# An encoder trunk on one core: the recurrence's squares summed before PE, row loads and top-k begun earlier, and the last tile's output on two engines

## The chip, the core and the metric

The kernel runs on one core of a Trainium2 chip. PE multiplies matrices, DVE and ACT work elementwise, POOL (GpSimd) here mostly issues gathers, SP issues loads and stores; the core shares 16 DMA engines among all of them. The metric is the time of one execution in microseconds (us). Before the change the median of three runs is 1483.56 us (1481.76 to 1483.88).

## What is computed

One layer of an encoder over 512 tokens of width 1024, all in 32 bits: a mixing stage (differential attention beside a two-way gated linear recurrence), a retrieval among 16384 small experts (8 heads, 16 experts each), a gate with a per-layer input, and a last norm. Cut to what matters:

```python
proj = rms_norm(h, norm_mix_g) @ w_in                       # q, k, v, lru_in, lru_gate
q = rope(q) * 64 ** -0.5; k = rope(k)
w = softmax(q0 @ k0.T) - lam * softmax(q1 @ k1.T)           # per head
attn = rms_norm(w @ v, diff_norm_g) * (1 - lambda_init)
rec = rms_norm((h_f + h_b) * gelu(lru_gate), lru_norm_g)    # norm over 512 channels
h = h + concat(attn, rec) @ w_out

xn = rms_norm(h, norm_ffn_g)
s1 = q_a @ keys1.T; s2 = q_b @ keys2.T                      # 128 keys each, per head
idx, sc = top 16 of the sums of the 16 best of s1 and of s2
act = gelu(xn . u[idx]) * softmax(sc)
h = h + sum over idx of act * v[idx]

h = h + sigmoid(rms_norm(h, norm_ple_g) @ w_gate) * (p @ w_proj)
out = rms_norm(h, final_norm_g)
```

## The kernel before

**Numbers.** A 32-bit product is made of three matmuls: each operand is split into a high part (ACT, L90) and the rest (DVE, L92, or L94 with a scale), and `mm3` (L97 to L99) multiplies high by high, high by low and low by high. So behind nearly each product stand one ACT and one DVE instruction for the split.

**Mixing stage (0 to some 240 us).** The tokens lie in 4 tiles of 128. A loop over 8 column blocks `ct` (L277) projects into the recurrence; in block 0 `x_norm` (L204) loads the four tiles of x and sums their squares on ACT, and `bcast_rows` spreads the four rstd columns: a DVE instruction each makes `dg` (L110), a PE matmul against ones puts it into `psr` (L111), and ACT copies it to `rb`, which every block's evacuation needs. Then the loop over `blk` (q, k, v) and `k2` (a quarter of the weights each) makes q, k and v, while the recurrence runs on DVE and ACT in its shadow; behind blk 1's products the rotation of q and k (L434 to L445) stands. In blk 2, `rec_out` (L361) makes the recurrence's norm: 16 matmuls of the squares `uc` against two columns of ones (`psq`, L369) give the sum over the channels, four `wo_load` calls (L350) load and split output weights, and `psb` takes the products. The attention loop (L545) has 16 steps, one per head and token tile: `scores` into `ps` (L472), the maximum of two 512-wide rows on DVE (L481) and its scaling by -0.125 (L482), the exponentials on ACT (L488), their combination on DVE (L494 to L496), four transposes into `pw` (L508), split into `wTh` and `wTl`, and the values into `pso`. Behind them the norms: squares summed by matmuls into `pq` (L525), `rd`, `dg` and `pb` again by `bcast_rows`, `ugz` (the normed values, L539), and the output product `psa`.

**Retrieval.** A loop over 8 heads (some 240 to 297 us) makes the queries. Then the u stage: 128 rows, each a load of 128 experts' u (`r`, 512 KB, SP queue L650), its split into `rh` and `rl`, and 24 matmuls of 384 columns (`psl`) for three of the four token tiles; ACT applies the gelu (`lg`). Beside each row, generators run in shares: `top` (top-k of the scores), `make` (`build`, the weights of the dense table, L808) and `side` (`rows`, which handles one token tile wholly by gathers from u and v on POOL, L888, with DVE products, L920 and L927). A constant per row (L43, L44) says how much of each generator is written behind a row. `settle` closes the pools of this stage, and the v stage follows: 128 rows again, `acc` matmuls of 512 columns with `am`, split into `ah` and `al`. From row `PREP` on, `prepare` loads the last stage's weights. `finish` (L1137) does the gate and the output norm, a token tile at a time.

**What sets the order.** The order of each engine's instructions is fixed when the kernel is built, from the order of writing, the needs of each instruction and a few manual dependencies; a buffer of a pool is reused when its readers are done. Nothing is reordered on the chip by need: an instruction that waits holds up what is queued behind it on its engine.

Of the kernel before, what the change touches and what calls it, by code (L numbers as in the profile page):

```python
# [11 lines left out]
F32 = mybir.dt.float32  # L12
# [10 lines left out]
P = 128  # L23
D = 1024
DK = D // P
T = 512
# [16 lines left out]
TOP_FIRST, TOP_THEN, MAKE, SIDE_1, SIDE, BG_V, PREP, SIDE_2 = 1.9, 1.0, 0.57, 0.85, 1.2, 1.2, 60, 2.1  # L43
MAKE_2, REST = 0.62, 3  # L44
# [16 lines left out]
def trunk(ctx, tc, x, xT, pT, pos, w_lru, w_qkv, w_out, w_q, keys, wab, w_gate, w_proj,  # L61
# [85 lines left out]
    with ExitStack() as st:  # L147
# [129 lines left out]
        for ct in range(8):  # L277
            wh, wl = wnext
            if ct < 7:
                wnext = lru_w(ct + 1)  # L280
            if ct == 0:
                x_norm()
            ps = mm.tile([P, T], F32, tag="mm", name="ps")
            for k in range(DK):
                mm3(ps, wh[:, k, :], wl[:, k, :], xgh[:, k, :], xgl[:, k, :], k == 0, k == DK - 1)
            if ct == 0:
                psr = psb.tile([P, T], F32, tag="tr", name="psr", bufs=2)
                bcast_rows(wk, psr, [rstd[:, 0, t:t + 1] for t in range(NT)])
                nc.scalar.copy(rb, psr)
# [30 lines left out]
        late_mix = []  # L320
# [29 lines left out]
        def wo_load(k):  # L350
# [7 lines left out]
            split(w, woh, wol)  # L358
            return woh, wol

        def rec_out():  # L361
# [4 lines left out]
            psq = psb.tile([P, T], F32, tag="ro", name="psq", bufs=1)  # L366
# [4 lines left out]
            nc.vector.tensor_copy(sq8[:, 0:8], psq[:, 0:8])  # L371
            rsqrt_mean(rstd[:, 1, :], sq8[:, 0:8].rearrange("p (t two) -> p t two", two=2)[:, :, 0], 512)
            nc.scalar.activation(warm, warm, AF.Exp)
            wr_ = []
            for k in range(4):
                wr_.append(wo_load(4 + k))
                yield
# [14 lines left out]
        rg = recurrence()  # L392


        for blk in range(3):
# [9 lines left out]
            for k2 in range(4):  # L405
# [19 lines left out]
                if blk == 2:  # L425
                    for _ in range(2):
                        next(ro)
            for t in range(NT):
# [5 lines left out]
                if blk == 1:  # L434
                    g = qk[:, t, :].rearrange("p (g d) -> p g d", d=64)
                    x1, x2 = g[:, :, 0:8], g[:, :, 8:16]
# [140 lines left out]
        for k in (2, 3):  # L577
            wa_.append(wo_load(k))
# [733 lines left out]
```

## Time and profile before

| what | value |
|---|---|
| median of the runs | 1483.56 us (1481.76 to 1483.88) |
| the profiled execution, its own time | 1491.43 us |
| its span, first to last instruction | 1489.7 us |
| PE busy | 1462.2 us, 98% |
| DVE busy | 1246.7 us, 84% |
| ACT busy | 737.3 us, 49% |
| POOL busy | 375.3 us, 25% |
| mean granted TensorE clock | 0.993 |
| DMA, mean over the span | 264 GB/s, 392.64 MB |

The profiled execution is one run and took longer than the median. A busy share is an average over stages with different limits, so it has to be read by stage: which engine is full there, and which wait ends last. The granted clock says how much of full speed PE was given in a stretch.

### The profile page before, as it was taken

The page shows a single profiled execution, that of the slowest core. Times are in us where ns is not written, and L with a number is a line of the kernel's source. Part 1 is how long each engine was busy: PE and PEld are TensorE (multiplying, and loading weights), DVE is VectorE, ACT ScalarE, POOL GpSimd, SP SyncE. Part 2 cuts the span into 40 slices and gives each one's busy share as a digit, 9 for nine tenths or more (in the row PEclk, how much of TensorE's full clock was granted, in tenths as well). Part 3 has the DMA queues.
Part 4 walks back from the last instruction along what each step waited for, and adds up shares of the span by engine and source line. Part 5 has one row for each costly group of instructions (what it writes and reads, how often), then busy time and mean ns, then how long its engine had stood idle before and what let it go on. Part 6 is the DMA issues. An engine that isn't in the chain of part 4 may idle for free.

```text
span 1489.7 us, 22160 instructions
## 1 busy us (share of the span) xinstructions
PE 1462.2 (98%) x7907; PEld 1294.2 (87%) x7907; DVE 1246.7 (84%) x2382; ACT 737.3 (49%) x1059; POOL 375.3 (25%) x320
## 2 busy tenths in 40 slices
PE   9999999999999999999999999999999999999997
PEld 7888678899999999999999997888888888888876
DVE  7686986798999998999888777888887568988896
ACT  7974654253455665556455533333333553333346
POOL 0000000002222263333433352232222004344350
PEclk9999999999999999999999999999999999999999
DMA  7134012158788899888997899899999789999962
GB/s 259 59 97 128 14 62 97 46 166 290 247 289 314 306 338 326 305 320 306 345 360 274 286 364 330 294 332 320 360 359 347 253 267 335 370 375 379 345 205 78
DMA packets 168047, 392.64 MB, mean 264 GB/s; under 512 B 15232, under 2 KB 89728, under 8 KB 164864
## 3 DMA queue, kind: packets, MB, share of 16 engines
q1 hardware_dynamic: 111760, 206.74, 41.0%
q0 software_dynamic: 38464, 140.00, 26.5%
q10 hardware_dynamic: 17712, 44.48, 7.8%
q8 instruction: 62, 1.02, 0.3%
q14 instruction: 49, 0.40, 0.1%
HBM read 344.63 MB, written 46.53 MB: 263 GB/s over the span
## 4 chain that ended last, share of the span: by engine, by line
PE 71%; DVE 14%; issue 5%; DMA 5%; ACT 4%; POOL 1%; SPq 0%; DVEq 0%; POOLq 0%; ACTq 0%
PE acc L99 11%; PE acc L98 11%; PE acc L97 11%; PE psl L97 7%; PE psl L99 7%; PE psl L98 7%; DVE rl L92 3%; PE pg L849 2%; PE ps L97 2%; PE ps L99 2%; PE ps L98 2%; DVE h L927 1%; DMA rr<-in_u_dram,qidx 1%; DMA r<-in_v_dram 1%; DVE rr L920 1%
## 5 line engine op out<-in xcount | busy, mean ns | idle before, releaser
L90 ACT ACTIVATE rh<-r 128x1024 fp32r<-128x1024 f32 x256 | 271.2, 1060 | 460.2 <-PE psl L98 190.2
L92 DVE TENSOR_TENSOR rl<-r,rh 128x1024 fp32r<-128x1024 f32 x256 | 312.4, 1221 | 104.0 <-ACT rh L90 103.3
L97 PE MATMUL psl<-x2h,rh 128*128 128x384 f32 x1024 | 346.8, 339 | 1.1 <-ACT lg L661 0.8
L99 PE MATMUL psl<-x2h,rl 128*128 128x384 f32 x1024 | 343.3, 335 | 2.6 <-DVE rl L92 2.6
L98 PE MATMUL psl<-x2l,rh 128*128 128x384 f32 x1024 | 343.0, 335 | 0.0
L97 PE MATMUL acc<-rh,ah 128*128 128x512 f32 x768 | 299.9, 391 | 2.5 <-ACT ah L90 2.5
L99 PE MATMUL acc<-rh,al 128*128 128x512 f32 x768 | 300.1, 391 | 1.2 <-DVE al L92 1.2
L98 PE MATMUL acc<-rl,ah 128*128 128x512 f32 x768 | 299.6, 390 | 0.0
L888 POOL DMA_INDIRECT rr<-in_u_dram,qidx x84 | 109.0, 1298 | 356.6 <-DVE rl L92 284.9
L99 PEld LDWEIGHTS psl<-x2h,rl 128*128 128x128 f32 x1024 | 192.4, 188 | 3.3 <-DVE rl L92 3.3
L97 PEld LDWEIGHTS psl<-x2h,rh 128*128 128x128 f32 x1024 | 192.2, 188 | 1.6 <-ACT lg L661 1.1
L98 PEld LDWEIGHTS psl<-x2l,rh 128*128 128x128 f32 x1024 | 192.6, 188 | 0.0
L888 POOL DMA_INDIRECT rr<-in_v_dram,qidxv x82 | 123.5, 1507 | 222.6 <-DVE rl L92 185.8
L97 PEld LDWEIGHTS acc<-rh,ah 128*128 128x128 f32 x768 | 144.7, 188 | 33.6 <-ACT ah L90 3.8
L99 PEld LDWEIGHTS acc<-rh,al 128*128 128x128 f32 x768 | 144.5, 188 | 32.7 <-DVE al L92 3.1
L98 PEld LDWEIGHTS acc<-rl,ah 128*128 128x128 f32 x768 | 144.6, 188 | 30.1
L920 DVE CUSTOM_DVE_ANT_0 rr<-rr,xn 128x1024 f32<-128x1024 f32 x84 | 102.0, 1217 | 8.7 <-DMA rr<-in_u_dram,qidx 8.7
L927 DVE SCALAR_TENSOR_TENSOR h<-rr,qg,h 128x1024 f32<-128x1024 f32 x82 | 104.9, 1279 | 0.1
L852 ACT COPY sg<-pg 128x512 f32<-128x512 f32 x96 | 96.0, 1109 | 6.4 <-PE pg L849 5.5
L888 POOL DMA_INDIRECT xn<-in_v_dram,qidxv x46 | 68.6, 1492 | 118.5 <-DVE rl L92 107.9
L90 ACT ACTIVATE ah<-am 128x384 fp32r<-128x384 f32 x128 | 65.6, 513 | 53.9 <-DVE am L1061 27.8
L888 POOL DMA_INDIRECT xn<-in_u_dram,qidx x44 | 62.8, 1427 | 113.0 <-DVE rl L92 82.4
(338 smaller groups left out, 2215.5 us busy)
## 6 DMA issues: line engine op xcount, KB each, us to landing
r<-in_ut_dram SPq DMA_DIRECT2D x128, 512.0 KB, 4.7
r<-in_v_dram SPq DMA_DIRECT2D x128, 512.0 KB, 6.8
gd<-sg ACTq DMA_DIRECT2D x24, 1024.0 KB, 7.8
gc<-gd SPq DMA_DIRECT2D x128, 192.0 KB, 5.0
ld<-lg ACTq DMA_DIRECT2D x98, 192.0 KB, 5.4
lg<-ld SPq DMA_DIRECT2D x98, 192.0 KB, 6.5
w<-in_w_qkv_dram SPq DMA_DIRECT2D x12, 512.0 KB, 3.6
w<-in_w_out_dram SPq DMA_DIRECT2D x8, 512.0 KB, 3.7
```

The costliest lines, as they stand in the source:

```text
L90: nc.scalar.activation(hi, src, AF.Copy, scale=1.0 if scale is None else scale)
L92: return nc.vector.tensor_sub(lo, src, hi.bitcast(F32))
L97: nc.tensor.matmul(ps, lhsT=lh, rhs=rh, start=first, stop=False)
L98: nc.tensor.matmul(ps, lhsT=lh, rhs=rl, start=False, stop=False)
L99: nc.tensor.matmul(ps, lhsT=ll, rhs=rh, start=False, stop=last)
L849: nc.tensor.matmul(pg[:, i - q, :], lhsT=o1[:, i // 2, :, i % 2], rhs=o2[part][:, i // 2, :, i % 2], start=part == 0, stop=part == 1)
L852: nc.scalar.copy(sg[:, :, s0:s0 + 4].rearrange("p j t -> p t j"), pg)
L888: g = nc.gpsimd.indirect_dma_start(out=dst, out_offset=None, in_=table, in_offset=bass.IndirectOffsetOnAxis(ap=idx, axis=0))
L920: behind(nc.vector.tensor_tensor_reduce(rr, rr, xn[:, t, :], 1.0, 0.0, ALU.mult, ALU.add, act[:, k % 16:k % 16 + 1]))
L927: behind(nc.vector.scalar_tensor_tensor(h[:, t, :], rr, qg[:, t, k:k + 1], h[:, t, :], op0=ALU.mult, op1=ALU.add))
```

## The change

It has six parts. (1) In the first loop the evacuation of a block becomes `lru_rest`; `x_norm` and `psr` move from block 0 to block 1, block 0's result waits in `first`, and on SP one weight load goes ahead of the four loads of x. (2) In `rec_out` DVE adds the four channel blocks of the squares (two additions, 1024 and 512 columns), and `psq` has 4 matmuls in place of 16, written behind the weight loads; the rotation of q and k moves from behind blk 1 into blk 2's loop, a token tile per quarter. (3) In attention q is split with the scale -0.125, so that DVE takes the minimum of the scores and no scaling follows; the exponential has the scale -1. (4) Behind attention the splits of two weight loads are ordered behind the last `wTl`, each next to the norm of a head, and the loads of the first two query weights stand one tile later. (5) In the retrieval, top-k of tile 0 takes a step per head in the heads loop, and the first three row loads are issued there; its generators yield `None`, which ends a row's share, before and after work that goes to ACT; the shares change; the gathers' buffers are held free for `prepare` from row `PREP` - 8 on (`hold`). (6) The last tile's output: the gain is multiplied in while the later columns are still on PE, and the last scale is made by ACT for one half and by DVE for two quarters.

```diff
-TOP_FIRST, TOP_THEN, MAKE, SIDE_1, SIDE, BG_V, PREP, SIDE_2 = 1.9, 1.0, 0.57, 0.85, 1.2, 1.2, 60, 2.1
-MAKE_2, REST = 0.62, 3
+TOP_FIRST, TOP_THEN, MAKE, SIDE_1, SIDE, BG_V, PREP, SIDE_2 = 2.1, 1.08, 0.62, 1.1, 1.23, 1.2, 60, 1.7
+MAKE_2, REST = 0.74, 3
...
+        def lru_rest(ct, ps):
...
+            if ct == 1:
+                x_norm()
...
+            if ct == 1:
+                psr = psb.tile([P, T], F32, tag="tr", name="psr", bufs=2)
+                bcast_rows(wk, psr, [rstd[:, 0, t:t + 1] for t in range(NT)])
+                nc.scalar.copy(rb, psr)
+            if ct == 0:
+                first = ps
+                continue
+            if ct == 1:
+
+                lru_rest(0, first)
+            lru_rest(ct, ps)
...
-            split(w, woh, wol)
+            lo = split(w, woh, wol)
+            if k >= 2 and k < 4:
+                tc.add_manual_dep(lo.ins, last_turn[-1].ins.name,
...
-            for t in range(NT):
-                for ct in range(4):
-                    nc.tensor.matmul(psq[:, 2 * t:2 * t + 2], lhsT=uc[:, ct, t * P:(t + 1) * P], rhs=ones[:, 0:2],
-                                     start=ct == 0, stop=ct == 3)
...
+                if k == 2:
+
+                    nc.vector.tensor_add(uc[:, 0:2, :], uc[:, 0:2, :], uc[:, 2:4, :])
+                    nc.vector.tensor_add(uc[:, 0, :], uc[:, 0, :], uc[:, 1, :])
+                if k == 3:
+                    psq = psb.tile([P, T], F32, tag="ro", name="psq", bufs=1)
+                    for t in range(NT):
+                        nc.tensor.matmul(psq[:, 2 * t:2 * t + 2], lhsT=uc[:, 0, t * P:(t + 1) * P], rhs=ones[:, 0:2],
+                                         start=True, stop=True)
...
-                split(pt, qkh[:, s, :], qkl[:, s, :])
+
+                split(pt, qkh[:, s, :], qkl[:, s, :], scale=None if s else -0.125)
...
-            nc.vector.reduce_max(sm[:, 0:2], ps, axis=AX.X)
-            nc.vector.tensor_scalar(sm[:, 2:4], sm[:, 0:2], -0.125, None, op0=ALU.mult)
+            nc.vector.tensor_reduce(sm[:, 2:4], ps, axis=AX.X, op=ALU.min)
...
-        for k in (2, 3):
-            wa_.append(wo_load(k))
         normed(2)
+        wa_.append(wo_load(2))
         squares(3)
         norms(3, 4)
         normed(3)
+        wa_.append(wo_load(3))
...
+        yield None
         nc.scalar.activation(g, g, AF.Exp)
+        yield None
...
+        if hd:
+            next(tks[0])
+        if hd >= HEADS - 3:
+            ahead.append(row_load(feed.pop(0)))
...
+                    if hold and turn_ < 0:
+
+                        break
...
+        if nq > 2:
+            a, b, c = (slice(*x_) for x_ in cuts)
+            nc.scalar.activation(sg[:, a], sg[:, a], AF.Copy, scale=sm[:, 1:2])
+            nc.vector.scalar_tensor_tensor(sg[:, c], h[:, t, c], sm[:, 1:2], gains[1][:, c], op0=ALU.mult, op1=ALU.mult)
+            nc.vector.tensor_scalar(sg[:, b], sg[:, b], sm[:, 1:2], None, op0=ALU.mult)
```

**Where the instructions stand.** On PE, in the v block of the projections: `wh` and `wl` with a number are the split weights of one quarter, `pst` their product, `psb` that of the recurrence's output. Before:

```order
L97 MATMUL pst<-wh_1014,xgh 128x512
L98 MATMUL pst<-wl_1015,xgh 128x512
L99 MATMUL pst<-wh_1014,xgl 128x512
L369 MATMUL psq<-ones,ugz 128x2 x16
L97 MATMUL pst<-wh_1099,xgh 128x512 x4
L97 MATMUL psb<-wo_1059,rec 128x512
L98 MATMUL psb<-wo_1059,rec 128x512
L99 MATMUL psb<-wo_1059,rec 128x512
L97 MATMUL psb<-wo_1059,rec 128x512
```

and after:

```order
L97 MATMUL pst<-wh_1105,xgh 128x512
L98 MATMUL pst<-wl_1106,xgh 128x512
L99 MATMUL pst<-wh_1105,xgl 128x512
L387 MATMUL psq<-ones,ugz 128x2 x4
L97 MATMUL pst<-wh_1165,xgh 128x512
L98 MATMUL pst<-wl_1166,xgh 128x512
L97 MATMUL psb<-wo_1031,rec 128x512
L98 MATMUL psb<-wo_1031,rec 128x512
L99 MATMUL psb<-wo_1031,rec 128x512
```

The squares' matmuls stood behind the first quarter's products and stand behind the third's.

On DVE, behind the last attention steps: `rd` and `s_` are the norms' sums, `dg` the operands of PE's `pb` matmuls, `wTl` the last split that the values wait for, `wol` and `wl` the low halves of output and query weights. Before:

```order
L387 SCALAR_TENSOR_TENSOR h<-psb,rstd,h 128x512
L92 TENSOR_TENSOR wTl<-pw,wTh 128x4x128
L92 TENSOR_TENSOR wol<-w,woh 128x1024
L534 RECIPROCAL rd<-rd 128x12
L531 SCALAR_TENSOR_TENSOR s_1245<-s_1245 128x4
L110 TENSOR_SCALAR dg<-ident,rd 128x128 x2
L92 TENSOR_TENSOR wol<-w,woh 128x1024
L110 TENSOR_SCALAR dg<-ident,rd 128x128 x3
L539 TENSOR_TENSOR ugz<-ugz,pb 128x512
L110 TENSOR_SCALAR dg<-ident,rd 128x128 x2
L527 COPY rd<-pq 128x4
```

and after:

```order
L402 SCALAR_TENSOR_TENSOR h<-psb,rstd,h 128x512
L549 SCALAR_TENSOR_TENSOR s_1235<-s_1235 128x4
L552 RECIPROCAL rd<-rd 128x12
L110 TENSOR_SCALAR dg<-ident,rd 128x128 x2
L92 TENSOR_TENSOR wTl<-pw,wTh 128x4x128
L110 TENSOR_SCALAR dg<-ident,rd 128x128 x2
L92 TENSOR_TENSOR wol<-w,woh 128x1024 x2
L92 TENSOR_TENSOR wl<-w,wh 128x1024
L557 TENSOR_TENSOR ugz<-ugz,pb 128x512
L110 TENSOR_SCALAR dg<-ident,rd 128x128 x2
```

Two pairs of `dg` now stand ahead of the weights' splits; the third pair stands behind three of them and the product `ugz`.

On DVE at the end of the v stage: `h` is a step of the gathered tile (L927 before, L974 after), `x_` the normed tile 3, `hl` the split of its transposes. Before:

```order
L927 SCALAR_TENSOR_TENSOR h<-rr,qg,h 128x1024
L1173 SCALAR_TENSOR_TENSOR sg<-h,sm,gains 128x512
L927 SCALAR_TENSOR_TENSOR h<-xn,qg,h 128x1024
L1162 TENSOR_TENSOR sg<-sg,pp 128x512
L1173 SCALAR_TENSOR_TENSOR sg<-h,sm,gains 128x512
L102 TENSOR_SCALAR sm<-sm 128x1
L1163 TENSOR_TENSOR h<-h,sg 128x512
L1162 TENSOR_TENSOR sg<-sg,pp 128x512
L1163 TENSOR_TENSOR h<-h,sg 128x512
L104 RECIPROCAL sm<-sm 128x1
L1144 SCALAR_TENSOR_TENSOR x_14075<-h,sm,gains 128x1024
L1170 TENSOR_REDUCE sm<-sm 128x1
```

and after:

```order
L974 SCALAR_TENSOR_TENSOR h<-xn,qg,h 128x1024
L1201 TENSOR_TENSOR sg<-sg,pp 128x512
L1202 TENSOR_TENSOR h<-h,sg 128x512
L104 RECIPROCAL sm<-sm 128x1
L1221 SCALAR_TENSOR_TENSOR sg<-h,sm,gains 128x512
L102 TENSOR_SCALAR sm<-sm 128x1
L1221 SCALAR_TENSOR_TENSOR sg<-h,sm,gains 128x512
L104 RECIPROCAL sm<-sm 128x1
L1183 SCALAR_TENSOR_TENSOR x_14050<-h,sm,gains 128x1024
L1201 TENSOR_TENSOR sg<-sg,pp 128x512
L1202 TENSOR_TENSOR h<-h,sg 128x512
L92 TENSOR_TENSOR hl<-turn,hl 128x512 x2
```

Between the last gathered step and `x_` stood five instructions of 512 columns, and four stand there now; `hl` follows `x_` behind four others before and behind two now.

## Rows read from the trace of the kernel before

**Rows 1.** The page, part 1: busy us, share of the span, instructions.

```profile
PE 1462.2 (98%) x7907; PEld 1294.2 (87%) x7907; DVE 1246.7 (84%) x2382; ACT 737.3 (49%) x1059; POOL 375.3 (25%) x320
```

**Rows 2.** Stretch: us, busy us of PE, PEld, DVE, ACT, POOL; clock; DMA share, GB/s.

```profile
0.00:30.00 30.00, 26.55 (x111) 20.66 (x112) 20.11 (x57) 21.98 (x34) 2.10 (x17) 1.00 0.84 304
108.00:130.00 22.00, 21.44 (x97) 17.98 (x96) 19.35 (x45) 12.47 (x19) 0.00 (x0) 0.84 0.39 126
160.00:200.00 40.00, 39.05 (x227) 27.41 (x226) 39.64 (x86) 29.68 (x72) 0.00 (x0) 1.00 0.12 39
204.00:222.00 18.00, 15.62 (x69) 12.70 (x68) 14.21 (x33) 8.59 (x13) 1.73 (x33) 0.81 0.18 60
240.00:297.00 57.00, 56.03 (x315) 48.70 (x314) 38.86 (x139) 19.75 (x33) 0.00 (x0) 1.00 0.20 65
...
600.00:700.00 100.00, 99.59 (x702) 97.61 (x700) 99.29 (x245) 59.32 (x75) 31.32 (x20) 1.00 0.88 314
888.00:912.00 24.00, 20.71 (x83) 15.84 (x83) 16.99 (x28) 6.48 (x10) 8.66 (x7) 0.93 1.01 373
```

**Rows 3.** Waits in 0 to 30: engine, line, releaser: us, times, longest.

```profile
PE ps L99 <- DVE wl L92: 1.0, 2, 0.6
...
PE psr L111 <- DVE dg L110: 0.5, 1, 0.5
```

**Rows 4.** The chain of waits in 105 to 130: start us, us, what.

```profile
110.84 1.15 DVE wl L92
...
117.58 4.56 PE psq L369 x32
...
125.34 0.43 PE psb L97
...
127.34 0.23 PE pst L99
```

**Rows 5.** Groups of lines in 130 to 210, and who waited for L482.

```profile
L92 DVE TENSOR_TENSOR wTl<-pw,wTh 128x512 fp32r<-128x512 f32 x16 | 11.0, 686 | 0.9 <-ACT wTh L90 0.8
...
L482 DVE TENSOR_SCALAR sm<-sm 128x2 f32<-128x2 f32 x16 | 2.6, 161 | 0.1
...
  ACT pe L488: 4.3, 6
```

**Rows 6.** PE's timeline in 200 to 220: start, us, operation, [idle <- releaser].

```profile
205.03 0.51 PE L97 MATMUL pso<-wTh,vhl 128*128 128x512 f32 x1 [0.73 <-ACT wTh L90]
...
210.26 0.71 PE L111 MATMUL pb<-dg,ones 128*128 128x128 f32 x4 [1.26 <-DVE dg L110]
```

**Rows 7.** PE's waits in 297 to 888, and the row split on the page.

```profile
PE psl L99 <- DVE rl L92: 2.6, 2, 1.4
PE pg L849 <- DVE o L834: 1.5, 2, 1.3
PE psl L97 <- ACT lg L661: 0.8, 1, 0.8
...
L92 DVE TENSOR_TENSOR rl<-r,rh 128x1024 fp32r<-128x1024 f32 x256 | 312.4, 1221 | 104.0 <-ACT rh L90 103.3
```

**Rows 8.** Chain and waits in 885 to 915; DMA queues in 860 to 912.

```profile
885.05 0.17 PE psl L99
...
888.94 15.64 DMA r<-in_v_dram
...
ACT rh L90 <- DMA r<-in_v_dram: 10.9, 2, 5.5
...
q0 software_dynamic: 2823, 10.28, 52.3%
q1 hardware_dynamic: 6112, 8.70, 47.6%
```

**Rows 9.** Waits in 1425 to 1490, and the chain there.

```profile
PE gate L97 <- DVE hl L92: 1.4, 1, 1.4
...
1485.00 0.75 DVE sg L1173
```

More of the change, by code (lines that the diff above doesn't have):

```diff
@@ L376, in rec_out @@
                 wr_.append(wo_load(4 + k))
+                if k == 2:
[6 more added lines that the diff above has]
+                                         start=True, stop=True)
+                    nc.vector.tensor_copy(sq8[:, 0:8], psq[:, 0:8])
+                    rsqrt_mean(rstd[:, 1, :], sq8[:, 0:8].rearrange("p (t two) -> p t two", two=2)[:, :, 0], 512)
+                    nc.scalar.activation(warm, warm, AF.Exp)
                 yield
@@ L508, in turn @@
                 nc.tensor.transpose(pw[:, kt, :], pe[:, 0, kt * P:(kt + 1) * P], ident)
-            split(pw, wTh[:, :, qt * P:(qt + 1) * P], wTl[:, :, qt * P:(qt + 1) * P])
+            last_turn.append(split(pw, wTh[:, :, qt * P:(qt + 1) * P], wTl[:, :, qt * P:(qt + 1) * P]))
         oT, osq = uc, gz
@@ L598, in trunk @@
         banks.append([psb.tile([P, T], F32, tag=g, name="psa", bufs=1) for g in ("ro", "po")])
-        wq = [wq_load(hd) for hd in range(2)]
         x2h = xp.tile([P, DK, T], R, tag="xa", name="x2h")
@@ L605, in trunk @@
             att_out(t, banks[t], (2, 3) if t < 2 else (0, 1, 2, 3))
+            if t == 0:
+                wq = [wq_load(hd) for hd in range(2)]
             for n in range(2):
@@ L787, in topk @@
         nc.vector.tensor_sub(bqh, tph, bq)
+        m2 = spread(i2h)
         yield 2.6
@@ L857, in trunk, with advance @@
     res = {t: [] for t in range(NT)}
+    tks = {t: topk(t, res[t]) for t in range(NT)}
     def tops():
         for t in list(range(NT - 1, ND_V - 1, -1)) + list(range(ND_V)):
-            yield from topk(t, res[t])
+            yield from tks[t]
     tg = tops()
+    pace, after = [], []
+    JC = 8
+    J0 = (P - KEEP) // JC * JC
+    order = [(J0 + i) % P for i in range(P)]
+    feed = [ut[j].rearrange("p k e -> p (k e)") for j in range(P)] + [v[j * P:(j + 1) * P, :] for j in order]
+    ahead = []
+    def advance():
+        while feed and len(ahead) < 3:
+            ahead.append(row_load(feed.pop(0)))
     for hd in range(HEADS):
@@ L875, in trunk @@
             next(tg)
+        if hd:
+            next(tks[0])
+        if hd >= HEADS - 3:
+            ahead.append(row_load(feed.pop(0)))
     nx.close()
     bw = e0.enter_context(tc.tile_pool(name="bw", bufs=2, side="right", reuse_waits="tile"))
-    pace, after = [], []
     def behind(ins):
@@ L975, in trunk @@
     top, make, side = Background(tg), Background(builds()), Background(rest())
-    JC = 8
-    J0 = (P - KEEP) // JC * JC
-    order = [(J0 + i) % P for i in range(P)]
-    feed = [ut[j].rearrange("p k e -> p (k e)") for j in range(P)] + [v[j * P:(j + 1) * P, :] for j in order]
-    ahead = []
     kept = {}
-    def advance():
-        while feed and len(ahead) < 3:
-            ahead.append(row_load(feed.pop(0)))
     def weights(c, part, vp):
@@ L1020, in trunk @@
         else:
-            if j == P - KEEP:
+            while j == P - KEEP and not top.done:
                 top.run(1e9)
@@ L1026, in trunk @@
                     if vp is None:
-                        make.run(1e9)
+                        while not make.done:
+                            make.run(1e9)
                         vp, wt, acc = settle()
@@ L1045, in trunk @@
     if vp is None:
-        make.run(1e9)
+        while not make.done:
+            make.run(1e9)
         vp, wt, acc = settle()
@@ L1167, in finish @@
             nc.scalar.activation(sg[:, ns], h[:, t, ns], AF.Square, accum_out=sm[:, 2 + q:3 + q])
+            if nq > 2 and q < nq - 1:
+                nc.vector.tensor_mul(sg[:, ns], h[:, t, ns], gains[1][:, ns])
             yield 1.2
```

103 lines of the change are left out of this document (51 added, 52 removed).

## Prediction

> **What bounds the kernel now.** I read the page's totals first, then a table by stretch, then for each stretch in which PE isn't full the waits and the chain. PE is busy 98% of the span [rows 1], and the chain of waits is mostly PE, so a gain can only come from four things: matmuls that go, time in which PE waits, time at the lower granted clock, and the tail behind the last matmul. All four are small. The table by stretch [rows 2] shows where they sit: 3.45 us of PE idle in 0 to 30 (30.00 less 26.55), a granted clock of 0.84 in 108 to 130, 0.81 in 204 to 222 and 0.93 in 888 to 912, and 3.3 us idle in 888 to 912. A mean clock of 0.84 over 22 us is a loss of 22 x 0.16 = 3.5 us at the full level; the other two come to 18 x 0.19 = 3.4 and 24 x 0.07 = 1.7. The chain shows the two levels: a 512-column matmul steps by 0.43 us at one and 0.23 at the other [rows 4], 1.2 and 2.4 GHz. In the u stage (297 to 888) PE waits only 4.9 us in five waits [rows 7], although DVE is full there, 99.29 of 100 in 600 to 700 [rows 2]. This is the point to keep in mind: DVE has no room there, and the change moves DVE work about.
>
> **The start** (x's norm and the broadcast of rstd one column block later). No work goes; the four psr matmuls, and the four DVE instructions that make their operands, come some 22 matmuls later in PE's order. PE now waits 0.5 us in psr and 1.0 us for wl, which stands behind psr's operands in DVE's queue [rows 3]. 22 matmuls are 5 us by the 0.23 of [rows 4], more than both waits. I take 0.5 and 0.8 of the 1.0: -1.3. Ends: 0 (x lands later too, since a weight load now goes ahead of its four loads on SP) and -2.0. The first block's evacuation waits for rb; PE goes on with the second block, whose psum is another buffer, so I count nothing.
>
> **The squares' sum over the recurrence's channels.** The 16 psq matmuls take 4.56 us for 32 records in the chain [rows 4], 4 of them a quarter of it, so 3.4 go. The matmuls right behind it still step by 0.43, those from 127 on by 0.23 [rows 4], so the clock falls in or by this run of two-column matmuls. With four of them between full ones I expect no fall: 3.5, of which I take 0.8 as lying in psq's 4.56 already, so 2.7. Against this stand two adds on DVE of 1024 and 512 columns, 1.2 + 0.7 us by L92's row [rows 7] and the wTl rows of the same width [rows 5], and the rope, now inside the same loop. DVE is busy 19.35 of 22 us here [rows 2], and it hands PE the low halves of the weights, as at 110.84, when PE waited for one [rows 4]. I take two thirds of the adds' 1.9 as new waiting for such a half, 1.3; the ends are 0 and 2.5. Together -3.4 - 2.7 + 1.3 = -4.8; ends -6.1 and -0.9 (the fall stays, later).
>
> **Attention.** DVE is busy 39.64 of 40 us in 160 to 200 [rows 2], so here DVE sets the pace and PE follows. The 16 scalings of the maxima go, 16 x 0.161 = 2.6 us [rows 5]; the minimum reads as many elements as the maximum did, and I count no difference. The split of q has a scale now: 0.75 by the instruction with a scale of [rows 9] instead of 0.69 by wTl's [rows 5], four times, 0.2. Net -2.4 of DVE in a stage that is DVE's for most of its length: -2.0; ends 0 (its last part waits for ACT) and -4 (ACT's exponentials waited 4.3 us for these scalings [rows 5]).
>
> **The norms behind attention.** Before, PE waited 0.73 for wTh and 1.26 for dg, and the clock fell soon after [rows 6]. The change puts two dg pairs ahead of the weights' splits, which removes the 1.26. But the third pair now stands behind wol, wol, wl (3 x 1.22) and one 512-wide product (0.7): 4.4 us from the second pair to it. PE has until then eleven pso, two pb and four pq matmuls, 2.5 + 0.25 + 0.5 = 3.2 us. A wait of about 1.2 comes back, one place later, and with it, more likely than not, the fall. So I take -0.5; ends +1 and -5 (1.5 of waits and the 3.4).
>
> **The heads of the retrieval.** Tile 0's top-k steps move into this stage: one per head, seven in all, some 9 us of DVE work by the number of instructions. DVE is busy 38.86 of 57 us there [rows 2]; PE has its matmuls beside it. Three row loads are issued here too; the DMA share is 0.20. I take 0, ends -1.5 and +3: one u row that comes late.
>
> **The u stage.** The background's shares per row rise (top-k 1.9 to 2.1 and 1.0 to 1.08, the builds 0.57 to 0.62; only the side work's last one falls), and by the order the builds end at row 114 instead of 120. Total DVE work is the same. Of PE's five waits, the ACT one of 0.8 should go, since topk's Exp and build's spread copies now end that row's share and so no longer stand ahead of the row's own ACT work. The two for rl may stay or grow. I take 0; ends -4 and +3.
>
> **Settle** (the end of the u stage). Here one row load took 15.64 us, and ACT waited 10.9 us for row loads in all [rows 8]; PE then waited for ah and al, idle 3.3, and lost 1.7 to the clock. The DMA share is 1.01 [rows 2]: gathers (the software queue, q0) have 52.3% and the loads of SP (q1) 47.6% in 860 to 912 [rows 8]. With settle six rows earlier, the order shows 1.45 gathers per row where there were 2. I take -3 of the 5.0; ends 0 and -6.3 (with 1.3 of smaller gaps).
> The Trainium skill bears on this, page "DMA: Bandwidth & Descriptors", section "Issuing engines are not separate DMA queues": DMAs of all issuing engines run on the same 16 DMA engines and interleave. By that rule only the bytes in the stretch matter; a quarter of 52.3% fewer is 13%, 2.0 us of the 15.64, and the term would be -2, the sum -11.4. No run here shows it apart.
>
> **Preparation and end.** The last row work ends nearer to the last v row: 15 h rows behind the last row split instead of 19, and tile 3's x3 and hl splits stand earlier on DVE. PE waited 1.4 for hl there [rows 9]; but the transposes of tile 3 stand earlier too, so a new wait eats most of it: -0.4. The last tile's output was two DVE instructions in a row, 0.75 each [rows 9]; now ACT has one half and DVE two quarters, so about 0.4 goes. Together -0.8; ends 0 and -2.5.
>
> **How the numbers follow.** -1.3 - 4.8 - 2.0 - 0.5 + 0 + 0 - 3 - 0.8 = -12.4. The profiled execution took 1491.43, the median is 1483.56, 0.5% less; no row says where the 7.9 lie, so I apply the sum to the median unscaled: **1471.2, say 1471**. A measurement of this kernel can tell about 0.2% (3 us) from no change.
>
> **Rivals.**
> *The falls stay.* PE gets the same number of waits at other places, and the clock falls at each. Then psq gives 3.4 - 1.3 = 2.1, settle at most 1.5, and with the start, attention and the end (4.1) the gain is 7.7 at most: 1476 to 1480.5. For it: one of the two early falls comes right behind waits of PE [rows 6], and the order keeps one there. Against: psq's own run is cut to a quarter.
> *More goes.* All falls go and the u stage loses its waits: 12.4 + 4.5 (norms) + 3.3 (settle) = 20, or 23 with half the u stage's: 1460 to 1464. Against: the dg pair behind 4.4 us of DVE work.
> *The change gives nothing.* What the front gains, PE waits for in the u stage, where DVE is full: gain under 3, 1480.6 to 1486.5.
> *Slower, by DVE in the u stage.* A row's low half rl (1.22 us [rows 7]) stands in DVE's queue behind the background of that row. In 600 to 700 DVE had 0.71 us free [rows 2], so higher shares have no room there. A u row takes PE 24 matmuls of 0.17 us [rows 8], 4.1 us, some 24 rows in 100 us; 0.25 us more DVE per row is 6 us in 100. Below some 4 us in all, a lead of DVE over PE by one row covers it. From 16 us (0.25 us in each of 64 rows) it outweighs the 12.4, and the time is 1483.56 - 12.4 + 16 = 1487; at 0.3 us it is 1490. For it: both rl waits already exist. Against: the builds end only six rows sooner, 5%, and in the order the DVE work between two rl is nearly unchanged.
>
> **Chances.** 1466 to 1476: 0.46. Falls stay, 1476 to 1480.6: 0.23. More goes, under 1466: 0.14. Nothing: 0.10. Slower: 0.07. So faster by over 0.2% 0.83, within 0.10, slower 0.07. The range leaves out 0.04 below 1460 and 0.14 above 1482.
>
> **What would show it.** Right: psq's group at 8 records and a granted clock of 1.00 around it; PE waits in 0 to 30 under 2.3; the stretch of attention 2 us shorter; a row load of under 8 us behind settle; the last output 0.4 us sooner behind the last reciprocal. Wrong: waits of PE for rl in the u stage above 6 us in all; a granted clock still near 0.84 or 0.81 ahead of the retrieval; a row load of 15 us that has only moved with settle.

## The result: slower by 0.84%, and the profile after

The changed kernel takes 1498.09 us (median of 5, 1494.73 to 1500.08) beside 1483.88 for the kernel before (1481.76 to 1486.16): a ratio of 1.0084, interval 1.0067 to 1.0101. The forecast was 1471, faster. Its profiled execution took 1497.94 us, its span is 1496.2, 6.5 more than the span before.

The first part of the page, and the busy times by stretch (us of PE, PEld, DVE, ACT, POOL; clock; DMA share, GB/s), of the changed kernel:

```profile
PE 1459.6 (98%) x7883; PEld 1292.2 (86%) x7883; DVE 1248.7 (83%) x2370; ACT 734.1 (49%) x1057; POOL 384.0 (26%) x320
```

```profile
0.00:30.00 30.00, 27.14 (x117) 21.75 (x118) 19.11 (x55) 21.73 (x33) 1.58 (x16) 1.00 0.80 293
108.00:130.00 22.00, 19.09 (x75) 14.69 (x74) 21.37 (x42) 13.91 (x19) 0.00 (x0) 0.92 0.44 144
160.00:200.00 40.00, 38.98 (x232) 27.85 (x230) 38.97 (x76) 29.61 (x73) 0.00 (x0) 1.00 0.13 44
204.00:222.00 18.00, 16.15 (x80) 13.37 (x81) 14.04 (x32) 6.36 (x12) 1.73 (x33) 0.91 0.19 61
240.00:297.00 57.00, 56.28 (x321) 49.45 (x321) 45.85 (x197) 20.96 (x37) 0.00 (x0) 1.00 0.20 66
600.00:700.00 100.00, 95.26 (x674) 92.91 (x673) 96.10 (x239) 59.00 (x73) 34.98 (x21) 1.00 0.88 313
888.00:912.00 24.00, 24.00 (x118) 21.20 (x118) 21.22 (x27) 9.29 (x15) 12.02 (x9) 1.00 1.00 359
1100.00:1130.00 30.00, 27.52 (x111) 21.13 (x109) 23.14 (x34) 12.56 (x17) 8.45 (x12) 0.94 1.02 357
1240.00:1260.00 20.00, 18.11 (x73) 14.46 (x73) 18.47 (x23) 6.35 (x9) 11.11 (x6) 0.91 1.04 386
```

Against [rows 1] PE is busy 2.6 us less in a span that is 6.5 us longer, so the loss is waiting. Against [rows 2] three things got better: 0 to 30 (27.14 for 26.55), the clock in 108 to 130 and 204 to 222 (0.92 and 0.91 for 0.84 and 0.81), and 888 to 912, where PE now has no gap. Worse are 600 to 700 (95.26 for 99.59) and two stretches of the v stage that were full before: 27.52 of 30 in 1100 to 1130 and 18.11 of 20 in 1240 to 1260, both with a fallen clock. These two in the kernel before:

```profile
1100.00:1130.00 30.00, 30.00 (x134) 24.86 (x133) 24.33 (x38) 10.91 (x15) 8.75 (x9) 1.00 1.03 373
1240.00:1260.00 20.00, 20.00 (x90) 16.58 (x89) 14.37 (x19) 6.62 (x10) 7.59 (x5) 1.00 1.05 384
```

DVE in 600 to 700 is busy 96.10, less than the 99.29 before: PE waits there while DVE isn't full.

PE's waits of the changed kernel, first in 297 to 890, then in 890 to 1420 (engine, line, releaser: us, times, longest):

```profile
PE pg L874 <- DVE o L859: 5.7, 2, 3.3
PE psl L97 <- ACT lg L680: 3.5, 1, 3.5
PE psl L99 <- DVE rl L92: 1.5, 2, 1.0
```

```profile
PE acc L98 <- DVE rl L92: 1.9, 1, 1.9
PE acc L97 <- ACT ah L90: 1.8, 1, 1.8
PE acc L99 <- DVE al L92: 1.4, 2, 0.8
```

10.7 us in the u stage stand against the 4.9 of [rows 7], and 5.1 in the v stage against 0.4 in 912 to 1425 before. The clock comes on top. In the u stage it fell in this stretch:

```profile
300.00:400.00 100.00, 96.48 (x545) 96.16 (x544) 87.13 (x317) 45.72 (x59) 19.77 (x16) 0.97 0.71 239
```

0.97 over 100 us is 3 to 3.5 more, so the u stage lost 9.2 us, and the v stage some 8 (0.06 x 30 + 0.09 x 20 = 3.6 more). Settle gave back its 5.0.

These are waits and clock alone; matmuls that went or changed their stage come beside them. PE's records give the parts of the span with everything in: the first product of the heads loop starts at 239.8 (242.4 before), the last at 291.9 (293.5), the first `acc` at 895.8 (890.3), the last `acc` at 1439.5 (1431.5), the last matmul at 1488.15 (1481.58). So the mixing stage is 2.6 us shorter, the heads loop 1.0 longer, the u stage 7.1 longer, settle and the v stage together 2.5 longer, the end 1.4 and the tail behind it 0.1 shorter: 6.5 in all.

The medians lie 14.2 apart and not 6.5, because the profiled execution of before took 7.5 us more than its median. Somewhat under half of this is the granted clock: it was 0.993 there, and the 23 executions of the kernel before beside the last two experiments have a mean of 0.9953, 19 of them 0.995 or more; 0.0023 of 1485 us is 3.4. No row places the rest. These 23 reach from 1480.41 us at a mean clock of 0.998 to 1491.71 at 0.992; 0.006 of 1485 us is 8.9 of these 11.3. The five of the changed kernel had 0.992 to 0.994.

### The profile page after: what moved, and what is told of

Its sections match the earlier page's. It is cut to its first block, busy times and chain, and to the rows that moved or that the text cites. A ratio compares the mean times of both kernels' runs of the same rounds, so it can differ in the third digit from the quotient of the medians.

```text
span 1496.2 us, 22103 instructions
## 1 busy us (share of the span) xinstructions
PE 1459.6 (98%) x7883; PEld 1292.2 (86%) x7883; DVE 1248.7 (83%) x2370; ACT 734.1 (49%) x1057; POOL 384.0 (26%) x320
## 4 chain that ended last, share of the span: by engine, by line
PE 70%; DVE 13%; issue 8%; ACT 5%; DMA 3%; POOL 1%; SPq 0%; DVEq 0%; POOLq 0%; ACTq 0%
PE acc L99 9%; PE acc L98 9%; PE acc L97 9%; PE psl L97 9%; PE psl L98 9%; PE psl L99 9%; PE pg L874 2%; DVE rl L92 2%; PE ps L97 1%; PE ps L99 1%; PE ps L98 1%; DMA rr<-in_v_dram,qidxv 1%; DVE h L974 1%; DVE o L859 1%; DVE rr L967 1%
## 5 line engine op out<-in xcount | busy, mean ns | idle before, releaser
L930 POOL DMA_INDIRECT rr<-in_u_dram,qidx x85 | 113.9, 1340 | 378.3 <-DVE rl L92 326.3
L930 POOL DMA_INDIRECT rr<-in_v_dram,qidxv x82 | 131.3, 1601 | 202.8 <-DVE rl L92 170.4
L974 DVE SCALAR_TENSOR_TENSOR h<-rr,qg,h 128x1024 f32<-128x1024 f32 x82 | 105.0, 1280 | 5.7 <-DMA rr<-in_v_dram,qidxv 5.6
L92 DVE TENSOR_TENSOR al<-am,ah 128x384 fp32r<-128x384 f32 x128 | 70.8, 553 | 33.9 <-ACT ah L90 33.3
```

The lines of the kernel that those rows point to most:

```text
L92: return nc.vector.tensor_sub(lo, src, hi.bitcast(F32))
L930: g = nc.gpsimd.indirect_dma_start(out=dst, out_offset=None, in_=table, in_offset=bass.IndirectOffsetOnAxis(ap=idx, axis=0))
L974: behind(nc.vector.scalar_tensor_tensor(h[:, t, :], rr, qg[:, t, k:k + 1], h[:, t, :], op0=ALU.mult, op1=ALU.add))
```

## The experiments

Three theories of the u stage: **S**, the larger shares per row make DVE late; **Y**, the new ends of shares put ACT's work where DVE isn't ready; **H**, the early top-k steps start the stage with a debt on DVE. Times are medians; ratios are against the kernel before on the same chip. PE's waits in 297 to 890 are the sums of the rows of PE's waits in one traced execution. Such a sum varies by itself: the changed kernel, e4 and e12 have the same u stage and show 10.7, 10.9 and 13.9 us, e8 and e14 have the same one and show 3.1 and 5.8. A difference of up to some 3 us tells nothing.

**What varies by itself.** `e1_before_again` is the kernel before, with no edit.

> The kernel before, unchanged, for a second profile. Its profiled execution took 1491.43 against a median of 1483.88, and the trace of it shows one stall of 6.3 us at the end of the u stage (a row load of 15.64 us). Theory A: that stall is of this one execution, so a second execution is near 1484, its row load there takes 5 to 9 us and PE is full in 885 to 912. Rival B: every execution has it and the profiler adds the rest; then the load takes 14 us or more again and the execution is near 1491.

1487.49 us at a clock of 0.994. The row load at settle took 13.91 us, and PE's waits in 850 to 915 came to 2.2 us instead of 3.3. So the late load belongs to the kernel, not to one execution; what differs between the executions is the clock (0.994, 0.993) and how much of the late load reaches PE.

**The mixing stage and the retrieval apart.** `e2_mixing` takes only the parts from the start to the norms; `e3_retrieval` only the generators, shares, early loads and the hold, as in the diff of the change.

> Only the parts in the mixing stage: x's norm one block later, the squares summed on DVE, the minimum in attention, the order behind attention. Theory A (the loss is in the retrieval): 1480 to 1483, since the new profile shows 1 to 3 us less from the start to 240 us. Rival B (the loss begins in the mixing stage, where new waits on wTh, 3.0, and wh, 1.9, appear): 1484 to 1488.

> Only the retrieval's part: shares, ends of shares around ACT's work, early top-k steps and row loads, and the gathers held back ahead of the last stage's loads. Theory A: 1497 to 1502, the whole loss. Rival B: 1487 to 1493, half of it.

`e2`: 1487.77, ratio 1.0006 (0.9991 to 1.002). `e3`: 1499.18, ratio 1.0065 (1.0045 to 1.0085), with 13.4 us of PE's waits in 297 to 890. The loss is the retrieval's, and the 8.6 us forecast for the mixing stage aren't there at all in the median. (The traced execution of e2, 1485.16, was the fastest of its ten.)

**The hold.** `e4_no_hold`, the changed kernel with

```diff
-        if i == PREP - 8:
-            hold.append(i)
```

> The changed kernel without the hold on the gathers' buffers ahead of the last stage's loads. Theory A: 1492 to 1495, since the stall of 6.0 us at 1100 to 1130 goes back to the 1.1 of before. Rival B (the loads of the last stage collide there anyway): 1497 to 1499.

1495.74, ratio 1.0044 (1.0017 to 1.007); the stall is still there, 31 us later (ACT splits that load at 1147.29, where it did at 1116.31), with ACT waiting 6.3 us for the same load. Both theories missed it: the hold only moves it.

**Shares and ends of shares.** `e5_exp_in_share` takes the two `yield None` around Exp out of the changed kernel. `e6_shares_before` gives it the shares of before:

```diff
-TOP_FIRST, TOP_THEN, MAKE, SIDE_1, SIDE, BG_V, PREP, SIDE_2 = 2.1, 1.08, 0.62, 1.1, 1.23, 1.2, 60, 1.7
-MAKE_2, REST = 0.74, 3
+TOP_FIRST, TOP_THEN, MAKE, SIDE_1, SIDE, BG_V, PREP, SIDE_2 = 1.9, 1.0, 0.57, 0.85, 1.2, 1.2, 60, 2.1
+MAKE_2, REST = 0.62, 3
```

`e8_shares_no_yields` has these shares and none of the new ends, `e11_no_yields` the new shares and none of the ends; in both, build's two spread copies on ACT go back to their old places, since the ends had moved them.

> The changed kernel, but topk's Exp stands again within a row's share (the two ends of a share around it are taken out). Theory Y (the ends of shares put Exp where DVE isn't ready): the stalls at 360 to 400 (6.5 us) and 660 to 700 (5.9) go to some 1 to 2 each, 1489 to 1492. Theory S (the larger shares make DVE late, wherever Exp stands): both stay or grow, 1496 to 1501.

> The changed kernel with the shares per row of the kernel before (all numbers of those two lines), and the rest as changed. Theory S: the stalls at 360 to 400 and 660 to 700 shrink to under 2 each, 1488 to 1492. Theory Y: they stay, 1496 to 1500.

> The changed kernel with the shares of before and without any of the new ends of shares (around Exp and around build's copies); early top-k and row loads, the hold and the mixing stage as changed. Theory S or Y: 1487 to 1491, both being gone. Theory H: 1494 to 1500.

> The changed kernel without any of the new ends of shares (around Exp and around build's copies), with its own, larger shares. Theory S (larger shares make DVE late): as slow as the changed kernel or slower, 1497 to 1503, with PE waiting 5 us or more for build's o. Theory Y (the ends of shares do it): 1488 to 1492.

| kernel | shares | ends of shares | PE's waits, 297 to 890 | time | ratio |
|---|---|---|---|---|---|
| after | new | new | 10.7 | 1498.09 | 1.0084 (1.0067 to 1.0101) |
| e5 | new | new, but not around Exp | 14.1 | 1496.04 | 1.0064 (1.0043 to 1.0086) |
| e11 | new | before | 14.3 | 1500.83 | 1.0108 (1.0076 to 1.0141) |
| e6 | before | new | 6.7 | 1501.43 | 1.0109 (1.0081 to 1.0137) |
| e8 | before | before | 3.1 | 1489.13 | 1.0022 (1.0011 to 1.0034) |
| before | before | before | 4.9 | 1483.88 | 1 |

PE's waits in 297 to 890 of e11 and then of e8:

```profile
PE pg L869 <- DVE o L854: 6.5, 5, 2.9
PE psl L99 <- DVE rl L92: 4.1, 2, 2.6
PE psl L97 <- ACT lg L680: 1.8, 1, 1.8
PE pg L869 <- ACT lg L680: 1.0, 1, 1.0
PE ptt L836 <- DVE e L793: 0.9, 2, 0.5
```

```profile
PE psl L97 <- ACT lg L680: 3.1, 1, 3.1
```

With the new shares PE waits 7 to 11 us for build's `o` and for `rl`, both DVE's, whatever the ends are (the changed kernel, e5, e11); with the old ones it waits for neither in e6 and e8, 1.9 in e14, and 4.1 in the kernel before. Theory S holds for the u stage, and Y falls for it: taking the ends out of the changed kernel doesn't lessen these waits (14.1 and 14.3 us beside 10.7 to 13.9 with them). But e6 is no faster for it, and its time lies outside both forecasts. With ends and without larger shares the generators get less far in a row: the builds end late (the last `pg` at 854.4, in e8 at 833.9), PE waits 2.8 for `keep` at 857, 5.5 in the v stage (3.7 before, with settle's end) and again for tile 3 at the end, 6.1 against 2.5. So neither part is good alone, and together they aren't either: with neither of them e8 is the best of the five with the rest of the change. Where e8's last 0.2% lies isn't shown. PE waits 10.6 us in 0 to 297 against 7.9, but e2 has the same mixing stage and no measurable loss; e8's ten executions have a mean clock of 0.9932 beside 0.9949 of the kernel before on that chip, and 0.0017 of 1487 us is 2.5.

**The early top-k.** `e7_no_early_topk` takes the step per head and the early row loads out of the changed kernel.

> The changed kernel without the early steps of top-k and without the early row loads in the heads loop. Theory H (the loss begins there: DVE starts the u stage late): the stalls from 360 on shrink, 1489 to 1493. Theories S and Y: they stay, some rows later, 1496 to 1500.

1493.62, ratio 1.0045 (1.0031 to 1.0059), 6.7 us of waits in 297 to 890; the stall at 380 is gone, one of 3.8 for `o` at 500 stands. H's forecast holds for the first stall alone, but the early steps have a part in the loss: without them the new shares cost less (6.7 us beside 10.7 to 13.9, and an interval below that of the changed kernel). This run takes out the steps and the early row loads together; which of the two it is wasn't separated.

**Attention and the squares, alone on the kernel before.** `e9_attention` takes the three edits of attention (q split with -0.125, the minimum, the exponential's scale), `e10_psq` the sum on DVE and the four matmuls, without moving the rotation. Each is a single execution, so only their traces are used here.

> The kernel before with only attention's part of the change: q split with the scale -0.125, the minimum in place of the maximum and its 16 scalings gone. Theory P (DVE's busy time sets the pace there, as predicted): PE's time beyond its matmuls in 140 to 200 falls from 9.7 to some 7.5 us. Rival L (the loop's chain of waits sets it, not DVE's sum): it stays at 9 to 10, and DVE is only less busy.

> The kernel before with only the sum of the squares on DVE and the 4 psq matmuls behind the weight loads, the rotation of q and k where it was. Theory R (the rotation, moved into the same loop, makes DVE and ACT late with the weights' halves): no wait for wh there and the stretch from 100 to 140 is 3 to 5 us shorter than before. Rival D (the two adds alone do it): PE waits 2 us or more for wh or wl, and the stretch is shorter by at most 2.

ACT's timeline in 196 to 206 of e9 (start, us, operation):

```profile
201.29 2.00 ACT L90 ACTIVATE woh<-w 128x1024 fp32r<-128x1024 f32 x2
203.31 1.28 ACT L533 ACT_TABLE_LOAD   x1
204.60 0.21 ACT L533 ACTIVATE rd<-rd 128x12 f32<-128x12 f32 x1
204.72 0.58 ACT L90 ACTIVATE wTh<-pw 128x512 fp32r<-128x512 f32 x1
```

DVE is busy 39.02 of the 40 us from 160 to 200 where it was 39.64, and the last exponential starts 2.7 us earlier than before (197.35 for 200.01). But the first maximum already starts 2.2 earlier (148.11 for 150.28), with nothing edited ahead of it; the fall of the clock in 110 to 130 was half as long in this execution. So the loop itself is 0.5 us shorter (49.24 for 49.73), not 2.4, and rival L has the better of it. The row of a scaling says why its removal is worth so little. DVE's timeline of the kernel before:

```profile
173.04 0.16 DVE L482 TENSOR_SCALAR sm<-sm 128x2 f32<-128x2 f32 x1
173.11 0.16 DVE L494 RECIPROCAL sm<-sm 128x1 f32<-128x1 f32 x1
```

The scaling's record lasts 0.16 us, but the next instruction starts 0.07 behind its start: records overlap, and in 12 of the 16 places the step is 0.06 to 0.08. 16 x 0.07 is 1.1 us, not 2.6.

The last `wTh` starts at 204.72, where it was 204.39 before: it stands behind two weight splits, a table load and a square root on ACT. PE's wait for it is 3.0, where [rows 6] have 0.73. What the stage had gained comes back in one wait. In e10, PE's waits in 80 to 240:

```profile
PE pst L98 <- DVE wl L92: 4.7, 2, 4.1
PE pb L111 <- DVE dg L110: 1.4, 2, 1.3
PE pst L97 <- ACT wh L90: 0.8, 1, 0.8
```

4.7 us for `wl`, where 0.6 was before, and 0.8 for `wh`: D holds, and the stretch isn't shorter at all (the first maximum of attention starts at 152.13, 1.9 later than before). With the rotation moved, which R blamed, e2 and e18 wait 2.9 us for `wh` and `wl` instead of 5.5. They also have the later start of x's norm, so the move alone isn't shown. The clock fell in e10 too, right behind this wait.

**ACT's queue at the last stage's loads.** `e12_late_splits`, the changed kernel with

```diff
                     yield 1.2
+                    yield 1.2
+                    yield 1.2
-                    for g_ in got:
-                        split(*g_)
+                    for src, hi, lo in got:
+                        a_ = nc.scalar.activation(hi, src, AF.Copy, scale=1.0)
+                        tc.add_manual_dep(a_.ins, pace[-1].ins.name,
...
+                        nc.vector.tensor_sub(lo, src, hi.bitcast(F32))
```

> The changed kernel with the four splits of the last stage's first loads written two rows later and ordered behind a row's split, so that ACT doesn't stand waiting for a load with rows queued behind it. Theory Q (ACT's queue order makes that stall): the stall of 6 us at 1100 to 1130 goes to under 1, 1491 to 1495. Rival N (the DMA engines are full there, so the rows' own loads are late): it stays above 3, 1496 to 1499.

1493.44, ratio 1.0048 (1.0031 to 1.0065). PE's waits in 890 to 1420:

```profile
PE acc L99 <- DVE al L92: 0.6, 1, 0.6
PE acc L97 <- ACT ah L90: 0.2, 1, 0.2
```

0.8 us, where it waited 5.1. Q holds: the DMA engines are as full as in the changed kernel (a share of 0.94 from 890 to 1420 in both), and the stall is gone.

**Towards a faster version.** `e13_mixing_end_late` is the retrieval of before with the changed mixing stage, the output on two engines and the late splits; `e14_shares_late` is e8 with the late splits; `e15_top_175` and `e16_top_165` are e14 with a first share of top-k of 1.75 and 1.65.

> The retrieval of the kernel before, with the changed mixing stage, the last tile's output on two engines, and the splits of the last stage's first loads two rows later. From the stage sums of the traces: mixing -1 to -3, end -0.5, the loads -0.7: 1481 to 1485 beside a kernel before of 1486 to 1487. Rival: the mixing stage is worth nothing in many runs, 1485 to 1488.

> The run with the shares of before and none of the new ends of shares (early top-k and row loads kept), and the splits two rows later. Its stall of 4 us at 1100 to 1130 should go: 1484 to 1487, one stall of 4.7 us at 377 left. Rival: another stall takes its place, 1488 to 1491.

> As the run before it, with top-k's first share 1.75 in place of 1.9, which puts Exp of tile 0 a row later on ACT (behind 18 rows' lg and not 17). Theory K (the early steps end tile 0's top-k when DVE is at its least lead over PE, so a later Exp waits less): the stall at 377 falls from 4.7 to 2 to 3, 1483 to 1486. Rival: it only moves a row, 1485 to 1488.

> As before, with 1.65, which puts Exp two rows later (behind 19). Theory K: a stall under 1.5 there, but the builds end at row 118 as before the change, so some of settle's stall of 4 to 6 us comes back: 1483 to 1488. Rival: the stall moves on with Exp, 1487 to 1490.

1494.28 (1.0044), 1494.03 (1.0035), 1491.29 (1.0023, 1.0008 to 1.0037) and 1498.41 (1.0075): all four are slower than both of their forecasts. e15, PE's waits in 297 to 890 and in 1420 to 1496:

```profile
PE psl L97 <- ACT lg L680: 2.4, 2, 1.3
```

```profile
PE turn L1190 <- DVE x L1184: 6.5, 1, 6.5
...
```

and of e14 at the end:

```profile
PE turn L1190 <- DVE x L1184: 3.0, 1, 3.0
...
```

K holds for the stall in e15: in two stages of three it is the best of all, 2.4 us in the u stage and 0.6 in the v stage. But PE waits 6.5 us for tile 3's `x`. With the late splits the gathers' buffers, which the last stage's loads use too, come free two rows later by the kernel's text, and the gathered tile ends later: e14 differs from e8 in the late splits alone and has a wait of 3.0 for `x` where e8 has none, and e13 has one of 3.0 where e2 has none. The other 3.5 of e15 are no new delay: its PE comes to this point 8.9 us earlier than e14's (1458.2 for 1467.1), the gathered tile only 5.4 (1464.7 for 1470.1). In e12 this wait isn't there; that its larger side shares end the tile's work sooner is likely and wasn't tried apart. A stall in the v stage was exchanged for one at the end. In e13 the wait of 3.0 has a fall of the clock behind it that costs 2.5 us more than e2's in 1460 to 1480; 5.5 us is about what e13 is slower than e2 (1.0044 beside 1.0006). e16 shows that a smaller share isn't better by itself: it waits 8.0 us in the u stage, 5.2 of them for `rl`, and settle's stall, forecast to return, stays away (0.3 us in 850 to 915).

`e17_start_end` is the kernel before with x's norm one block later and the output on two engines; `e18_start_psq_end` has the squares' sum and the rotation's move as well.

> The kernel before with only two parts of the change: x's norm one block later, and the last tile's output on two engines. The terms of the prediction for these are -1.3 and -0.4. Theory T (both are real, nothing behind them is touched): 1484 to 1486 beside a kernel before of 1486 to 1487, and 1.3 us less of PE's waits in 0 to 40. Rival: the 1.3 come back later as waits for DVE or in the spread between executions, 1486 to 1488.

> The same with the squares summed on DVE and the rotation in the v block's loop, without attention's part and without the new order behind it. From the stage sums: psq's 2.7 of matmuls go, 1.3 of waits for wh and wl come: 1482.5 to 1485. Rival: 1486 to 1488, since the later clock falls and settle take it back.

`e17`: 1488.06, ratio 1.0022 (1.0006 to 1.0039). `e18`: 1485.2, ratio 1.0008 (0.9993 to 1.0023). e17's waits of PE in 0 to 140:

```profile
PE psq L376 <- ACT ugz L354: 2.1, 1, 2.1
...
PE ps L99 <- DVE wl L92: 0.6, 1, 0.6
```

The start is shorter (the waits for `psr` are gone; PE is 1.7 us ahead at 110), and a new wait of 2.1 us for the squares stands at `psq`; T's saving is real and comes back at once. e18 waits 2.9 for `wh` and `wl` as e2 does. No version here beats the kernel before; e18 and e2 can't be told from it.

## Why the prediction was wrong, step by step

**The u stage: the step that failed most.** The prediction set it to 0 with ends of -4 and +3, for "total DVE work is the same". The work is (DVE busy 1248.7 us for 1246.7), but the share of it ahead of a row isn't. It measured +9.2 by waits and clock, +7.1 by PE's records. The slower rival named the mechanism (DVE's background ahead of `rl`), and gave it 0.07, because the order showed the builds ending only 5% sooner. That was the wrong measure: PE's lead was eaten in single rows, and what PE waits for is `o` and `lg`, not `rl` alone: the prediction's own sign, over 6 us for `rl`, wasn't met (1.5). Larger shares do it together with the early top-k steps: with either taken away the waits are 3.1 to 6.7 us (e6, e7, e8, e14) and not 10.7 to 14.3. One sentence was wrong in its sign: that ACT's wait of 0.8 "should go". ACT's timeline in 360 to 386 of the changed kernel:

```profile
369.46 0.47 ACT L680 ACTIVATE lg<-psl 128x384 f32<-128x384 f32 x1
...
370.32 1.28 ACT L759 ACT_TABLE_LOAD   x1 [0.39 <-ACT lg L680]
378.31 0.31 ACT L759 ACTIVATE qg<-qg 128x128 f32<-128x128 f32 x1 [6.71 <-DVE qg L756]
378.63 1.28 ACT L680 ACT_TABLE_LOAD   x1
379.93 0.49 ACT L680 ACTIVATE lg<-psl 128x384 f32<-128x384 f32 x1
```

Exp waits 6.71 us for DVE's `qg`, and behind it in ACT's queue stands `lg`, which frees the product's buffer for PE. What ended ACT's idle time ahead of Exp, in its four places, before and after:

```profile
  DVE qg L737: 4.7, 2
  DVE qg L756: 12.1, 3
```

Ending the share puts Exp into another row; it doesn't put it behind the end of DVE's work. Around each Exp stand two table loads of 1.28 us; the Trainium skill, page "ScalarE: Activation LUTs", section "What ACT_TABLE_LOAD costs", gives 1283 ns for one, and the trace agrees (1283 at each of the four places). They are small beside the wait.

**Preparation: +8 in a stage that the sum had at nothing.** For the v stage behind settle the prediction has no term but -0.4 at its end, with no reason given. The load of the last stage's first operand takes as long as before (7.64 us, 7.86 before), and ACT waits for it about as long. ACT's timeline there, of the kernel before and then of the changed one:

```profile
1149.04 0.63 ACT L90 ACTIVATE wg<-w 128x512 fp32r<-128x512 f32 x1 [5.93 <-DMA w<-in_pT_dram]
1149.58 0.51 ACT L90 ACTIVATE ah<-am 128x384 fp32r<-128x384 f32 x1
1149.99 1.04 ACT L90 ACTIVATE rh<-r 128x1024 fp32r<-128x1024 f32 x1
```

```profile
1116.31 0.63 ACT L90 ACTIVATE wg<-w 128x512 fp32r<-128x512 f32 x1 [6.34 <-DMA w<-in_pT_dram]
1116.84 1.04 ACT L90 ACTIVATE rh<-r 128x1024 fp32r<-128x1024 f32 x1
1117.79 0.51 ACT L90 ACTIVATE ah<-am 128x384 fp32r<-128x384 f32 x1
```

Before, `ah`, which PE needs first, stood right behind the split; now `rh` of a later row stands between. That is 1 us. PE waits 1.8 for `ah` and 0.6 for `al` there, and the clock falls behind it; e12, where ACT isn't held up, waits 0.8 us in the whole v stage and has no fall there. The stretch at 1240 to 1260 (1.9 for `rl` and a fall) has its like in e7, 3.1 for `rl` near 1260, and none in e12, where PE's waits in 890 to 1420 come to 0.8; what made it isn't settled.

**Settle: right, and undersized.** -3 was taken; PE's 3.3 of gaps and 1.7 of clock are both gone, -5.0. The DMA share there is 1.00 where it was 1.01, so the queues are about as full as before, and still no row load is late for PE; ACT waits 4.0 us for row loads in 860 to 925 instead of the 19.2 before. It is the retrieval's edits that do it: e2 and e18, with the retrieval of before, still wait 3.3 and 3.9 us between 850 and 915. Of these edits none is needed alone: without the hold (e4), the early row loads (e7) or the new ends (e11) PE waits for nothing there, and with the shares of before (e8) 0.5. The Trainium skill, page "DMA: Bandwidth & Descriptors", section "Issuing engines are not separate DMA queues", says that loads of all issuers interleave on the same 16 engines. That only bytes matter was the prediction's reading of it, and had given -2 from 13% fewer bytes. In 860 to 912 the engines moved 18.09 MB where it was 19.01, 5% less, and the gaps fell by 3.3 us: bytes alone don't tell which load comes late. What does isn't shown.

**The heads.** 0 was taken, and +1.0 measured by PE's records: the products of seven steps stand there now.

**The start: right in its size, worthless in time.** PE gets through 117 records in 0 to 30 instead of 111, and at 110 it is 1.5 us ahead (110.51 for 112.03 where it next waits for `wl`), near the -1.3. e17 shows where it goes: x's norm later makes the recurrence later, and `psq` waits 2.1 us for it. In the changed kernel the next wait, for `wh`, is 1.9.

**The squares: two terms failed.** The matmuls' -3.4 held: `psq`'s 32 records took 4.72 us, the 8 in e18 take 0.95. The new wait was 2.9 - 0.6 = 2.3, not 1.3 (within the ends of 0 and 2.5). And the fall of the clock didn't go with psq's run, it moved to the new wait. PE's timeline of the changed kernel:

```profile
117.91 0.96 PE L97 MATMUL pst<-wh,xgh 128*128 128x512 f32 x3 [1.88 <-ACT wh L90]
119.67 0.52 PE L98 MATMUL pst<-wl,xgh 128*128 128x512 f32 x1 [0.80 <-DVE wl L92]
120.00 0.61 PE L99 MATMUL pst<-wh,xgl 128*128 128x512 f32 x1
120.41 0.63 PE L98 MATMUL pst<-wl,xgh 128*128 128x512 f32 x1
```

From 120.0 on the matmuls step by 0.42 where the full level steps by 0.23 [rows 4], until 123: half as long as before. e2 has the same wait and the same fall, e18 the same wait (1.9 and 0.8) and none. So psq's short matmuls weren't the only cause, and the rival "the falls stay" had the better reading of this place. Start and squares together bring the first maximum of attention 2.5 us forward (147.79 for 150.28), of which the shorter fall is 1.7; -6.1 was taken.

**Attention: the wrong limit.** -2.0 was taken from DVE's 39.64 busy of 40. Two steps of it failed. The 16 x 0.161 us are the lengths of records that overlap with the next; the queue steps by 0.07, and the loop, from the first maximum to the last exponential, is 0.5 us shorter in the changed kernel as in e9. And this came back, since the end of the stage waited on ACT (3.0 for `wTh`). From the first maximum to the first product of the heads it is 92.15 us before and 91.98 after. The lower end of 0, "its last part waits for ACT", was the answer.

**The norms and the end.** The wait forecast for the third `dg` pair isn't there. Another is, in front of it: PE's waits in 196 to 240 are 4.1 us (3.0 for `wTh`, 0.8 for `ugz`, 0.3 for `x2h`) where they were 2.3, so +1.8 stands where -1.5 of waits was hoped for; the clock, 0.91 for 0.81 over 18 us, gives the 1.8 back. -0.5 was near, for the wrong reason. At the end PE waits 1.5 us instead of 2.5, and its part behind the last `acc` is 1.4 shorter where -0.4 was taken. The last output's -0.4 isn't there: DVE's last result stands 1.0 us behind the last reciprocal instead of 1.6, but the span ends 4.8 behind it instead of 4.9.

**The bridge from the profile to the median.** "No row says where the 7.9 lie": somewhat under half of it is the clock, 0.993 in that execution and mostly 0.995 or more in others; the rest stays open. Terms taken from the clock of one execution (3.5, 3.4 and 1.7 here) count events that other executions have in part or not at all.

## What to carry to other kernels

Where an engine is full for hundreds of rows, look at what it owes before each row and not at its sum: the same DVE work in other shares took PE's waits in the u stage from 3.1 and 5.8 us (e8, e14) to 14.3 here (e11). Ahead of each instruction that can wait (an Exp for DVE's sums, a split for a load), name what stands behind it in the same queue; moving it by two rows took waits of 4.3 us away here (5.1 to 0.8, e12), and gave one of 3.0 back at the end in e13 and e14. A gain in a stage counts only if the last wait of the next stage moves too. And price a removed instruction by the step to the next start in its queue, not by the length of its record.

## What the runs showed of the hardware that was not expected

Executions of one program on one chip differ mostly by the granted clock: of the kernel before, 1480.41 us at 0.998 and 1491.71 at 0.992, of which the clock makes 8.9 us. e18's execution at 0.998 shows a granted clock of 1.00 from 100 to 240, where the traces of before have two falls. Yet PE waits there 1.9 and 0.8 us for the weights, as in the changed kernel and e2, where the clock falls behind these waits. So the same wait has a fall behind it in one execution and none in another.

Records on one engine overlap: 0.16 us of a small DVE instruction cost its queue 0.07 (173.04 to 173.11 in the kernel before).
